# ScalarE's and VectorE's order fixed around the last gate's first group, and a later place for the third output quarter's turn

## The chip, the cores and the metric

One Trainium2 chip, one core of it. The metric is the device time of one execution in microseconds; the kernel before takes 816.92 us, the median of 3 runs (816.7 to 817.8). Five engines work side by side, each on its own list of instructions in its own order: TensorE (PE in the profile), VectorE (DVE), ScalarE (ACT), GpSimd (POOL) and SyncE (SP), which issues most DMAs. They wait for each other through semaphores.

## The reference

One layer of a decoder trunk on 256 tokens of width 2048, in float32:

```
h = rmsnorm(x);  u = h @ w_in            # 2048 x 12288, ten fields
ya = b_g * conv3(c_g * xa) * silu(za);   yb = headnorm(hgrn2(q, f, iv)) * silu(og)
m = sigmoid(ga) * (ya @ w_a_out) + sigmoid(gb) * (yb @ w_b_out)
x = x + m @ w_o
gate = sigmoid(rmsnorm(x) @ w_ple_gate)
x = x + gate * (p @ w_ple_proj)
return rmsnorm(x) * final_norm_g
```

What bears on the change are the last two products: `m @ w_o` (called O below) and `rmsnorm(x) @ w_ple_gate` (called PG), each 256 x 2048 by 2048 x 2048.

## The kernel before

**Products.** TensorE gets float32 accuracy out of three passes. Every operand is cut into a high part, rounded to the type the fast pass takes, and the low rest. `cut` (line 195 on ScalarE, line 196 on VectorE) makes `whi` = the rounded copy of `raw` and `wlo` = `raw` - `whi`; `put` (lines 319 and 320) does the same for the activations and gives `xh` and `xl`. Lines 1122 to 1124 are the three passes: whi with xh, wlo with xh, whi with xl. Each is a matmul of 128 x 128 by 512 columns.

**Items.** All weights stand in one list, `items`. An ordinary item is a piece of 256 x 512 weights: 2 slices of 128 rows x 2 halves of the tokens x 3 passes = 12 matmuls. The main loop takes one item per step, `pos`. A step first writes down the cut of the item `LEAD` = 3 places ahead (some more later on), then the 12 matmuls of its own item, then the DMA issues of loads still further ahead, and then advances every epilogue by one piece (`advance`). An epilogue (`ep_o`, `ep_pg` and so on) is a generator: whatever stands up to its next `yield` is written down in this step. So a `yield` more is one step later.

**Buffers of the cuts.** Pairs of whi and wlo come from two rings (`free_pair`): four pairs that serve all along and five more from a pool `late`, which opens at step `gate`. A cut into one of the four waits until TensorE is done with the item that had the pair.

**O and its epilogue.** O has four groups, one for each quarter of 512 output columns, 8 items each. `ep_o(j)` adds the two psum banks of quarter j to the residual x (line 879, VectorE, two instructions), squares it for the norm (line 880, ScalarE, two) and copies it with its blocks reordered (line 886, ScalarE, two). `turned` then turns the quarter, as PG needs the features on the partitions: four stores to DRAM (line 350, SyncE), one step later the load back (line 361, SyncE), `lag` steps later the block transpose (line 354, VectorE). `put` follows: four xh and four xl, one for each 128 features. So quarter j gives the slices 4j to 4j + 3 of `x1T`, the operand of PG.

**PG and its first group.** PG's first two column quarters are taken together, as one group of 14 items, which begins at step `gate`. Of the 8 slices of 256 features, six are taken plainly, with two items each. The slices 3 and 5 (`LATE_SEVEN`) are combined: seven block products in place of eight, from sums of the activations and of the weights. `late_sums` makes the activations' sums: line 747 joins xh and xl, line 790 makes four differences and sums, `cut` splits them into `shi` and `slo`. Slice 5 belongs to the third quarter of O, so its late sums follow that quarter's turn. `combine_late` makes the sums of the weights (line 747 on `raw`, the cuts `bhi`, `blo` and two more pairs); `settled` is the step of slice 5's item, the tenth of the group. The products P1, P5, P6, P7 stand in four psum banks called g, the corrections in four called s. `ep_products`, written down at step `settled` + 2, takes them out: line 756 copies P1 (ScalarE), lines 747, 758, 747 and 760 combine P6, P5 and P7 (VectorE). The fourth group of O is the one just ahead of `gate`, so its squares, its turn and the third quarter's late sums all fall into the first steps of PG.

**Order.** Where nothing else is said, the scheduler behind the kernel's program may move an engine's instructions past each other by its own estimate of times. `pinned(mark)` takes that freedom away for the two engines that make the cuts: from this step's instructions on, each of ScalarE's and each of VectorE's is tied behind the one written down before it. Line 1304 says for which steps. Before the change these are the steps from `begun` to `parked` + 8, earlier in the program, and `gate` to `settled`. The last steps of O and the steps behind `settled` are free.

Of the kernel before, what the change touches and what calls it, by code (L numbers as in the profile page):

```python
# [48 lines left out]
def hybrid_kernel(ctx, tc, xT, x, pT, prm, gfin, masks, w_in, w_a, w_b, w_o, w_pg, w_pp, out):  # L49
# [32 lines left out]
    def t4(tag="t4", bufs=None):  # L82
        bufs = bufs or {"tmp1": 8, "tmp2": 1, "tmp3": 5}[state["tmp"]]
        return pools[state["tmp"]].tile([P, 1024], F32, tag=tag, bufs=bufs, name=nm(tag))
# [4 lines left out]
    def sc(n, tag="sc", bufs=12):  # L89
        return small.tile([P, n], F32, tag=tag, bufs=bufs, name=nm(tag))  # L90
# [154 lines left out]
    gate = next(n for n, it in enumerate(items) if it["op"] == "x1T")  # L245
    settled = max(n for n, it in enumerate(items) if it["kind"] == "S")
    parked = next(n for n, it in enumerate(items) if it["kind"] == "A" and it["j"] == 3)
    begun = next(n for n, it in enumerate(items) if it["kind"] == "ga" and it["last"])
# [56 lines left out]
    def gain(base, k):  # L305
        return prm_t[:, base + k : base + k + 1]
# [5 lines left out]
    def put(op, k, src, scale=None):  # L312

        hi, lo = op[0][:, k, :], op[1][:, k, :]
        if scale is None:
            nc.scalar.activation(out=hi, in_=src, func=AF.Copy)
            nc.vector.tensor_tensor(out=lo, in0=src, in1=hi.bitcast(F32), op=ALU.subtract)
        else:
            nc.scalar.activation(out=hi, in_=src, func=AF.Identity, scale=scale)  # L319
            nc.vector.scalar_tensor_tensor(  # L320
                out=lo, in0=src, scalar=scale, in1=hi.bitcast(F32), op0=ALU.mult, op1=ALU.subtract
            )


    def rsqrt_of(ss, n, width, tag):

        v = sc(n, tag + "v", 2)
        nc.vector.tensor_scalar(
            out=v, in0=ss, scalar1=1.0 / width, scalar2=EPS, op0=ALU.mult, op1=ALU.add
        )  # L330
        r = sc(n, tag + "r", 2)
        nc.gpsimd.tensor_tensor(out=r, in0=v, in1=mhalf[:, :n], op=ALU.pow)
        return r

    def blocks(ap):

        return ap.rearrange("p (c b e) -> p c b e", b=4, e=32)

    def spread(ap, t):

        return ap.rearrange("p (b c t e) -> p t c b e", b=4, c=4, t=NT)[:, t]

    def to_dram(src, tag, bufs, queue=nc.sync):
        d = dram.tile([P, 4, T], F32, tag=tag, bufs=bufs, name=nm(tag))
        to = d.rearrange("(b i) a x -> a i b x", b=4)
        for a in range(4):
            queue.dma_start(out=to[a], in_=src[32 * a : 32 * a + 32, :].rearrange("i (b x) -> i b x", b=4))  # L350
        return d

    def square_turn(dst, src):
        nc.vector.transpose(
            out=dst.rearrange("p (k a e) -> p a k e", a=4, e=32), in_=src.rearrange("p (a k e) -> p a k e", a=4, e=32)
        )

    def turned(src, lag, dst=None, queues=(nc.sync, nc.sync)):
        d = to_dram(src, "turn", 3, queues[0])
        yield  # L360
        queues[1].dma_start(out=src, in_=d.rearrange("p a x -> p (a x)"))
        for _ in range(lag):
            yield
        dst = t4() if dst is None else dst
        square_turn(dst, src)
        return dst
# [507 lines left out]
    def ep_o(j, psum):  # L874
        xs = state["x"]
        src = t4()
        for t in range(NT):
            d = xs[:, t, j * CW : (j + 1) * CW]
            nc.vector.tensor_tensor(out=d, in0=d, in1=psum[t], op=ALU.add)
            nc.scalar.activation(  # L880
                out=src[:, t * CW : (t + 1) * CW], in_=d, func=AF.Square,
                accum_out=state["ss2"][:, t * 4 + j : t * 4 + j + 1],
            )
        x1 = src
        for t in range(NT):
            nc.scalar.activation(
                out=spread(x1, t), in_=blocks(xs[:, t, j * CW : (j + 1) * CW]), func=AF.Copy
            )
        x1 = yield from turned(x1, 3 if j < 3 else 7)
        for c in range(4):  # L890
            put(state["x1T"], j * 4 + c, x1[:, c * T : (c + 1) * T], gain(PRM_GPLE, j * 4 + c))
        for c in LATE_SEVEN:
            if c // 2 == j:
                yield
                yield from late_sums(c)
        if j == 3:
            tot = sc(2, "tot2", 1)
            nc.vector.tensor_reduce(
                out=tot, in_=state["ss2"].rearrange("p (t j) -> p t j", t=NT),
                axis=mybir.AxisListType.X, op=ALU.add,  # L900
            )
            state["rstd2"] = rsqrt_of(tot, NT, D, "r2")

    def late_sums(c):
        if "late sums" not in state:
            n = len(LATE_SEVEN)
            both = pair_of(pools["tmp3"], 1, ("shi", "slo"), n * 4 * P)
            state["late sums"] = tuple(v.rearrange("p (u s t) -> p u s t", u=n, s=4) for v in both)
        f = t4()
        F, Sv = f[:, :CW].rearrange("p (r b t) -> p r b t", r=2, b=2), f[:, CW:].rearrange("p (s t) -> p s t", s=4)  # L910
        hi, lo = (v[:, 2 * c : 2 * c + 2, :] for v in state["x1T"])
        add(F.rearrange("p r b t -> p r (b t)"), hi.bitcast(F32), lo.bitcast(F32))
        yield
        sums_of(F[:, 0, 0], F[:, 1, 0], F[:, 0, 1], F[:, 1, 1], [Sv[:, i] for i in range(4)])
        yield
        cut(*(v[:, LATE_SEVEN.index(c)] for v in state["late sums"]), Sv)
        yield
# [76 lines left out]
    def ep_last(t, halves):  # L994
# [7 lines left out]
    epilogues = {  # L1002
        "f": ep_f, "q": ep_q, "iv": ep_iv, "og": ep_og, "c": ep_c, "xa": ep_xa, "za": ep_za, "b": ep_b,
        "ga": ep_ga, "gb": ep_gb, "A": ep_a, "B": ep_bb, "O": ep_o, "PG": ep_pg, "PP": ep_pp,
    }

# [92 lines left out]
    def step(e):  # L1099

        a, v = state["splits"]
        with tc.issue_after(a), tc.issue_after(v):
            try:
                next(e)
            except StopIteration:
                active.remove(e)
# [66 lines left out]
    def pinned(start):  # L1173
        traced = nc.cur_bb.bb.instructions
        for engine in (i.engine for i in state["splits"]):
            chain = [i for i in traced[max(start - 400, 0) :] if i.engine == engine]
            fresh = {i.name for i in traced[start:]}
            for a, b in zip(chain, chain[1:]):
                if b.name in fresh:
                    tc.add_manual_dep(  # L1180
                        b, a.name,
                        mybir.DependencyInfo(mybir.DependencyClass.NoSync, mybir.DependencyReason.DATA),
                        reason="order",
                    )
# [6 lines left out]
    for pos, it in enumerate(items[:last_group]):  # L1191
        mark = len(nc.cur_bb.bb.instructions)
        kind, j, c, last = (it[n] for n in ("kind", "j", "c", "last"))
# [99 lines left out]
        if last and kind not in ("S", "C"):  # L1293
# [7 lines left out]
            if not (kind == "f" and j == 0):  # L1301
                active.append(epilogues[kind](j, psum))
                step(active[-1])
        if begun < pos < parked + 8 or gate <= pos <= settled:
            pinned(mark)


# [96 lines left out]
```

## Time and profile before

| what | us |
|---|---|
| runs | 816.92, 816.7, 817.8 |
| profiled execution, its own time | 817.08 |
| its span, first to last instruction | 815.3 |
| TensorE busy, all matmuls | 803.5 |
| VectorE busy | 606.2 |
| ScalarE busy | 462.8 |
| last matmul of 512 columns before the two end pieces begins | 794.65 |

The mean granted clock of TensorE is 0.996. A row of the timeline gives the start and length in us, the engine, the line, the operation with out<-in, how many such instructions follow each other, and in brackets the idle time ahead of the first with what ended it. A suffix q after an engine's name is its queue of DMA issues.

### The profile page before, as it was taken

The page shows a single profiled execution, that of the slowest core. Times are in us where ns is not written, and L with a number is a line of the kernel's source. Part 1 is how long each engine was busy: PE and PEld are TensorE (multiplying, and loading weights), DVE is VectorE, ACT ScalarE, POOL GpSimd, SP SyncE. Part 2 cuts the span into 40 slices and gives each one's busy share as a digit, 9 for nine tenths or more (in the row PEclk, how much of TensorE's full clock was granted, in tenths as well). Part 3 has the DMA queues.
Part 4 walks back from the last instruction along what each step waited for, and adds up shares of the span by engine and source line. Part 5 has one row for each costly group of instructions (what it writes and reads, how often), then busy time and mean ns, then how long its engine had stood idle before and what let it go on. Part 6 is the DMA issues. An engine that isn't in the chain of part 4 may idle for free.

```text
span 815.3 us, 10701 instructions
## 1 busy us (share of the span) xinstructions
PE 803.5 (99%) x4053; PEld 663.9 (81%) x4053; DVE 606.2 (74%) x780; ACT 462.8 (57%) x624; POOL 59.5 (7%) x58
## 2 busy tenths in 40 slices
PE   9999999999999999999999999999999999999995
PEld 6888888888888888888888888888888888877885
DVE  6746588767765498767679878878987656788962
ACT  7576476465555466456455555556545455665733
POOL 1000000001000000000021210201000000000280
PEclk9999999999999999999999999999999999999998
DMA  9988565648767555648799996996845769884822
GB/s 331 391 310 289 196 207 166 236 137 275 249 236 252 193 177 199 207 156 270 259 337 297 320 296 218 324 297 214 249 156 193 281 235 342 291 286 172 317 78 103
DMA packets 53811, 198.52 MB, mean 243 GB/s; under 512 B 6912, under 2 KB 16384, under 8 KB 40064
## 3 DMA queue, kind: packets, MB, share of 16 engines
q1 hardware_dynamic: 44352, 174.78, 60.8%
q0 software_dynamic: 6384, 16.25, 8.3%
q10 hardware_dynamic: 3024, 6.82, 2.5%
q8 instruction: 31, 0.51, 0.3%
q14 instruction: 20, 0.16, 0.1%
HBM read 184.19 MB, written 13.63 MB: 243 GB/s over the span
## 4 chain that ended last, share of the span: by engine, by line
PE 95%; issue 1%; DVE 1%; ACT 1%; POOLq 0%; POOL 0%; ACTq 0%
PE g L1122 27%; PE g L1124 27%; PE g L1123 27%; PE s L1123 4%; PE s L1124 4%; PE s L1122 4%; PE s L530 1%; ACT whi L195 0%; PE s L1014 0%; ACT xh L319 0%; DVE wlo L196 0%; PE s L631 0%; PE s L650 0%; PE s L649 0%; PE s L648 0%
## 5 line engine op out<-in xcount | busy, mean ns | idle before, releaser
L196 DVE TENSOR_TENSOR wlo<-raw,whi 128x1024 fp32r<-128x1024 f32 (+1 forms) x266 | 318.4, 1214 | 151.1 <-ACT whi L195 149.3
L195 ACT ACTIVATE whi<-raw 128x1024 fp32r<-128x1024 f32 (+1 forms) x266 | 274.0, 1049 | 201.4 <-PE g L1124 168.3
L1122 PE MATMUL g<-whi,xh 128*128 128x512 f32 (+1 forms) x676 | 260.0, 385 | 0.0
L1124 PE MATMUL g<-whi,xl 128*128 128x512 f32 (+1 forms) x676 | 259.7, 384 | 0.0
L1123 PE MATMUL g<-wlo,xh 128*128 128x512 f32 (+1 forms) x676 | 259.6, 384 | 0.0
L1122 PEld LDWEIGHTS g<-whi,xh 128*128 128x128 f32 x676 | 127.0, 188 | 25.2
L1124 PEld LDWEIGHTS g<-whi,xl 128*128 128x128 f32 x676 | 127.0, 188 | 25.1
L1123 PEld LDWEIGHTS g<-wlo,xh 128*128 128x128 f32 x676 | 127.0, 188 | 24.9
L1123 PE MATMUL s<-wlo,xh 128*128 128x512 f32 x136 | 53.1, 390 | 0.5 <-DVE wlo L196 0.5
L1124 PE MATMUL s<-whi,xl 128*128 128x512 f32 x136 | 53.0, 390 | 0.0
L1122 PE MATMUL s<-whi,xh 128*128 128x512 f32 x136 | 52.5, 391 | 0.5 <-ACT xh L319 0.4
L1123 PE MATMUL g<-wlo,mh 128*128 128x512 f32 x128 | 49.8, 389 | 0.0
L1124 PE MATMUL g<-whi,ml 128*128 128x512 f32 x128 | 49.8, 390 | 0.0
L1122 PE MATMUL g<-whi,mh 128*128 128x512 f32 x128 | 49.5, 389 | 0.0
L195 ACT ACTIVATE thi<-sA 128x1024 fp32r<-128x1024 f32 x15 | 15.9, 1062 | 32.3 <-DVE sA L747 20.1
L1122 PEld LDWEIGHTS s<-whi,xh 128*128 128x128 f32 x136 | 25.5, 188 | 6.4 <-ACT xh L319 0.8
L1123 PEld LDWEIGHTS s<-wlo,xh 128*128 128x128 f32 x136 | 25.5, 188 | 6.3 <-DVE wlo L196 1.0
L1124 PEld LDWEIGHTS s<-whi,xl 128*128 128x128 f32 x136 | 25.5, 188 | 5.5 <-DVE xl L320 0.2
L1124 PEld LDWEIGHTS g<-whi,ml 128*128 128x128 f32 x128 | 24.0, 188 | 5.2 <-DVE ml L830 0.3
L1122 PEld LDWEIGHTS g<-whi,mh 128*128 128x128 f32 x128 | 24.0, 188 | 5.0
L1123 PEld LDWEIGHTS g<-wlo,mh 128*128 128x128 f32 x128 | 24.0, 188 | 5.0
L1124 PE MATMUL g<-whi,ybTl 128*128 128x512 f32 x64 | 24.9, 389 | 0.0
(243 smaller groups left out, 981.6 us busy)
## 6 DMA issues: line engine op xcount, KB each, us to landing
raw<-in_w_in SPq DMA_DIRECT2D x66, 1024.0 KB, 4.9
raw<-in_w_o SPq DMA_DIRECT2D x16, 1024.0 KB, 6.0
sT<-in_w_in POOLq DMA_DIRECT2D x30, 512.0 KB, 9.2
raw<-in_w_in SPq DMA_DIRECT2D x28, 512.0 KB, 6.1
raw<-in_w_a SPq DMA_DIRECT2D x8, 1024.0 KB, 8.4
raw<-in_w_b SPq DMA_DIRECT2D x8, 1024.0 KB, 8.4
raw<-in_w_pg SPq DMA_DIRECT2D x16, 512.0 KB, 6.0
raw<-in_w_pg SPq DMA_DIRECT2D x8, 1024.0 KB, 6.9
```

Source lines behind the costliest of these rows:

```text
L195: a = nc.scalar.activation(out=hi, in_=src, func=AF.Copy)
L196: v = nc.vector.tensor_tensor(out=lo, in0=src, in1=hi.bitcast(F32), op=ALU.subtract)
L530: nc.tensor.matmul(out, X[:, 0, h, s], X[:, 1, h, t], start=True, stop=True, tile_position=(0, i * n))
L1122: nc.tensor.matmul(psum, oh, hi, start=first, stop=False)
L1123: nc.tensor.matmul(psum, oh, lo, start=False, stop=False)
L1124: nc.tensor.matmul(psum, ol, hi, start=False, stop=last)
```

## The change

Two lines. The third quarter (j = 2) gets six steps instead of three between the load back of its turn and its transpose, with the `put`s and the late sums behind it. And the second stretch of pinned steps grows at both ends: it begins six steps ahead of `gate` and ends two steps behind `settled`.

```
@@ -886,7 +886,7 @@
-        x1 = yield from turned(x1, 3 if j < 3 else 7)
+        x1 = yield from turned(x1, (3, 3, 6, 7)[j])
@@ -1301,7 +1301,7 @@
-        if begun < pos < parked + 8 or gate <= pos <= settled:
+        if begun < pos < parked + 8 or gate - 6 <= pos <= settled + 2:
             pinned(mark)
```

No instruction is added or removed on any engine; GpSimd's order is the same, SyncE's and TensorE's nearly so.

ScalarE, from the cut of step gate's own item on (`whi_5998` before, `whi_5986` now; then gate+1 and gate+2, and the last whi in both lists is gate+3's). `xh` is the third quarter's, the rows of lines 880 and 886 are the fourth's, `shi` is the late sums' cut. Before:

```order
L195 ACTIVATE whi_5998<-raw_5930 128x1024
L195 ACTIVATE whi_6021<-raw_5930 128x1024
L195 ACTIVATE whi_6039<-raw_5967 128x1024
L319 ACTIVATE xh_5648<-t_1034_5970,prm_t 128x256 x4
L880 ACTIVATE t_1046_6058,ss_958_5502<-xs 128x512 x2
L886 ACTIVATE t_1046_6058<-xs 128x4x4x32
L195 ACTIVATE shi_5819<-t_1037_5996 128x512
L886 ACTIVATE t_1046_6058<-xs 128x4x4x32
L195 ACTIVATE whi_6074<-raw_5967 128x1024
```

Now:

```order
L195 ACTIVATE whi_5986<-raw_5930 128x1024
L195 ACTIVATE whi_6005<-raw_5930 128x1024
L319 ACTIVATE xh_5648<-t_1041_6021,prm_t 128x256 x4
L195 ACTIVATE whi_6031<-raw_5967 128x1024
L880 ACTIVATE t_1046_6052,ss_958_5502<-xs 128x512 x2
L886 ACTIVATE t_1046_6052<-xs 128x4x4x32 x2
L195 ACTIVATE whi_6068<-raw_5967 128x1024
```

The third quarter's xh moved ahead of the cut of gate+2, and shi moved behind the cuts of gate+3 and gate+4 (the latter, `whi_6102`, is not shown).

VectorE at the same place, from the wlo of gate+1 (`wlo_6022`, `wlo_6006`). L354 and L320 are the third quarter's, L747 and L790 its late sums, L879 the fourth quarter's. Before:

```order
L196 TENSOR_TENSOR wlo_6022<-raw_5930,whi_6021 128x1024
L196 TENSOR_TENSOR wlo_6040<-raw_5967,whi_6039 128x1024
L879 TENSOR_TENSOR xs<-xs,g_5899 128x512
L879 TENSOR_TENSOR xs<-xs,g_5900 128x512
L354 STREAM_TRANSPOSE t_1034_5970<-t_1020_5883 128x4x8x32
L320 SCALAR_TENSOR_TENSOR xl_5649<-t_1034_5970,prm_t,xh_5648 128x256 x4
L747 TENSOR_TENSOR t_1037_5996<-xh_5648,xl_5649 128x512
L790 TENSOR_TENSOR t_1037_5996<-t_1037_5996 128x128 x4
L196 TENSOR_TENSOR slo_5820<-t_1037_5996,shi_5819 128x512
L196 TENSOR_TENSOR wlo_6075<-raw_5967,whi_6074 128x1024
L196 TENSOR_TENSOR wlo_6105<-raw_6014,whi_6104 128x1024
```

Now:

```order
L196 TENSOR_TENSOR wlo_6006<-raw_5930,whi_6005 128x1024
L354 STREAM_TRANSPOSE t_1041_6021<-t_1020_5883 128x4x8x32
L320 SCALAR_TENSOR_TENSOR xl_5649<-t_1041_6021,prm_t,xh_5648 128x256 x4
L196 TENSOR_TENSOR wlo_6032<-raw_5967,whi_6031 128x1024
L747 TENSOR_TENSOR t_1045_6050<-xh_5648,xl_5649 128x512
L879 TENSOR_TENSOR xs<-xs,g_5899 128x512
L879 TENSOR_TENSOR xs<-xs,g_5900 128x512
L196 TENSOR_TENSOR wlo_6069<-raw_5967,whi_6068 128x1024
L790 TENSOR_TENSOR t_1045_6050<-t_1045_6050 128x128 x4
L196 TENSOR_TENSOR wlo_6103<-raw_6002,whi_6102 128x1024
L196 TENSOR_TENSOR slo_5820<-t_1045_6050,shi_5819 128x512
```

The transpose moved from behind gate+2's wlo and the two L879 to ahead of gate+2's wlo; L790 and slo moved behind the wlo of gate+3.

ScalarE at the group's end: line 756 (P1 out of its bank), the fourth quarter's xh, the whi of slice 5's weight sums (`whi_6266`, `whi_6270`) and those of the next group, PG 2 (`whi_6333` to `whi_6380`). Before:

```order
L195 ACTIVATE whi_6223<-raw_6157 128x1024
L756 ACTIVATE t_1109_6359<-g_6080 128x512
L319 ACTIVATE xh_5648<-t_1087_6250,prm_t 128x256 x4
L195 ACTIVATE whi_6266<-raw_6138 128x1024
L195 ACTIVATE whi_6270<-raw_6138 128x1024
```

Now, the same piece, and further on where line 756 has gone:

```order
L195 ACTIVATE whi_6223<-raw_6157 128x1024
L319 ACTIVATE xh_5648<-t_1087_6250,prm_t 128x256 x4
L195 ACTIVATE whi_6266<-raw_6138 128x1024
L195 ACTIVATE whi_6270<-raw_6138 128x1024
...
L195 ACTIVATE whi_6355<-raw_6306 128x1024
L756 ACTIVATE t_1109_6359<-g_6074 128x512
L195 ACTIVATE whi_6380<-raw_6306 128x1024
```

Line 756 moved from ahead of the fourth quarter's xh to behind the third cut of PG 2; on VectorE the line 747 that follows it moved behind the wlo of that cut (`wlo_6356`), and lines 758 and 747 behind the next one.

## Prediction

> **What bounds the kernel now.** The page first. Its first part:
>
> ```profile
> PE 803.5 (99%) x4053; PEld 663.9 (81%) x4053; DVE 606.2 (74%) x780; ACT 462.8 (57%) x624; POOL 59.5 (7%) x58
> ```
>
> TensorE is the bound, and the 99% hides how well it is fed, since a matmul of 512 columns is shown 0.39 us long but follows the one ahead of it closer than that. So the table by stretches comes next, read by the count of matmuls behind PE's busy time (the columns: us, busy us and count of PE, PEld, DVE, ACT, POOL, then PE's clock, the share and GB/s of DMA):
>
> ```profile
> 720.00:725.00 5.00, 5.00 (x24) 3.99 (x22) 3.69 (x10) 4.53 (x11) 0.00 (x0) 1.00 0.37 125
> 725.00:730.00 5.00, 4.42 (x19) 3.15 (x18) 4.69 (x5) 5.00 (x7) 0.00 (x0) 1.00 0.94 309
> 745.00:750.00 5.00, 4.17 (x17) 2.42 (x15) 2.58 (x7) 3.83 (x7) 0.71 (x1) 1.00 0.00 0
> 750.00:755.00 5.00, 4.79 (x22) 3.88 (x22) 5.00 (x5) 5.00 (x6) 0.00 (x0) 1.00 0.44 144
> 755.00:760.00 5.00, 5.00 (x24) 4.14 (x23) 5.00 (x7) 2.02 (x3) 0.00 (x0) 1.00 0.96 362
> ```
>
> A full stretch shows 24 matmuls; 725 to 730 lacks 5, 745 to 755 lacks 7 and 2. The clock column stays at 1.00. The timeline of PE shows where they are missing, with the waits in brackets:
>
> ```profile
> 716.91 0.39 PE L1122 MATMUL s<-whi,xh 128*128 128x512 f32 x1
> ...
> 725.29 0.73 PE L1122 MATMUL s<-whi,xh 128*128 128x512 f32 x2
> 726.55 0.50 PE L1123 MATMUL s<-wlo,xh 128*128 128x512 f32 x1 [0.53 <-DVE wlo L196]
> ...
> 734.41 0.39 PE L1122 MATMUL s<-bhi,shi 128*128 128x512 f32 x1
> ...
> 747.22 0.50 PE L1122 MATMUL s<-whi,xh 128*128 128x512 f32 x1 [0.40 <-ACT xh L319]
> ...
> 749.37 0.51 PE L1122 MATMUL g<-whi,shi 128*128 128x512 f32 x1 [0.43 <-ACT whi L195]
> ...
> 750.32 0.73 PE L1122 MATMUL g<-whi,shi 128*128 128x512 f32 x2 [0.21 <-ACT whi L195]
> ```
>
> Item `gate` begins at 716.91. An ordinary item is 12 matmuls and takes 2.72 us (0.2267 each), as the two whi rows at 711.67 and 714.39 below show: each is let go when an item ends. Six items later, at 716.91 + 6 x 2.72 = 733.23, the first combined item should begin; it does at 734.41. **First loss: 1.18 us**, at item gate+3. Fourteen missing matmuls x 0.2267 are 3.17 us in all, so the **second loss is about 1.99 us**. The whole change can win 3.2 us, 0.4%, if the rest of the order holds.
>
> Why they happen is in the timelines of ScalarE and VectorE. ScalarE:
>
> ```profile
> 700.22 0.62 ACT L880 ACTIVATE t<-xs 128x512 f32<-128x512 f32 x1
> ...
> 702.02 1.04 ACT L195 ACTIVATE whi<-raw 128x1024 fp32r<-128x1024 f32 x1
> ...
> 711.67 1.06 ACT L195 ACTIVATE whi<-raw 128x1024 fp32r<-128x1024 f32 x1 [1.66 <-PE g L1124]
> 714.39 1.06 ACT L195 ACTIVATE whi<-raw 128x1024 fp32r<-128x1024 f32 x1 [1.66 <-PE g L1124]
> 719.10 1.71 ACT L319 ACTIVATE xh<-t,prm_t 128x256 fp32r<-128x256 f32 x4 [3.64 <-DVE t L354]
> 720.71 0.61 ACT L880 ACTIVATE t<-xs 128x512 f32<-128x512 f32 x1
> ...
> 724.20 3.89 ACT L195 ACTIVATE whi<-raw 128x1024 fp32r<-128x1024 f32 x4
> ...
> 746.17 0.60 ACT L756 ACTIVATE t<-g 128x512 f32<-128x512 f32 x1 [8.24 <-PE g L1124]
> 746.67 1.70 ACT L319 ACTIVATE xh<-t,prm_t 128x256 fp32r<-128x256 f32 x4
> 748.26 6.74 ACT L195 ACTIVATE whi<-raw 128x1024 fp32r<-128x1024 f32 x7
> 756.62 2.01 ACT L195 ACTIVATE whi<-raw 128x1024 fp32r<-128x1024 f32 x2 [1.61 <-DMA raw<-in_w_pg]
> ```
>
> VectorE:
>
> ```profile
> 712.77 1.23 DVE L196 TENSOR_TENSOR wlo<-raw,whi 128x1024 fp32r<-128x1024 f32 x1 [1.49 <-ACT whi L195]
> 715.49 1.23 DVE L196 TENSOR_TENSOR wlo<-raw,whi 128x1024 fp32r<-128x1024 f32 x1 [1.50 <-ACT whi L195]
> 716.63 1.28 DVE L879 TENSOR_TENSOR xs<-xs,g 128x512 f32<-128x512 f32 x2
> 717.83 1.24 DVE L354 STREAM_TRANSPOSE t<-t 128x1024 f32<-128x1024 f32 x1
> 719.64 1.68 DVE L320 SCALAR_TENSOR_TENSOR xl<-t,prm_t,xh 128x256 fp32r<-128x256 f32 x4 [0.58 <-ACT xh L319]
> 721.36 0.69 DVE L747 TENSOR_TENSOR t<-xh,xl 128x512 f32<-128x512 f32 x1
> 722.09 1.02 DVE L790 TENSOR_TENSOR t<-t 128x128 f32<-128x128 f32 x4
> 723.80 0.69 DVE L196 TENSOR_TENSOR slo<-t,shi 128x512 fp32r<-128x512 f32 x1 [0.70 <-ACT shi L195]
> 725.27 4.63 DVE L196 TENSOR_TENSOR wlo<-raw,whi 128x1024 fp32r<-128x1024 f32 x4 [0.78 <-ACT whi L195]
> ...
> 743.65 1.24 DVE L354 STREAM_TRANSPOSE t<-t 128x1024 f32<-128x1024 f32 x1
> 747.20 1.69 DVE L320 SCALAR_TENSOR_TENSOR xl<-t,prm_t,xh 128x256 fp32r<-128x256 f32 x4 [2.32 <-ACT xh L319]
> ```
>
> First loss: the cut of gate+3 (724.20, the first of four) stands behind the third quarter's turn, the fourth's squares and the late sums' shi; between 715.45 and 724.20 ScalarE cuts no weights, and PE wants that whi at 716.91 + 3 x 2.72 = 725.07. Second loss: L756 waits 8.24 us for the last product of P1, and the fourth quarter's xh, whose turn was done at 743.65 + 1.24 = 744.89, stands behind it until 746.67. The xh, the two whi of the last combined item and PE's waits at 747.22, 749.37 and 750.32 follow in one chain.
>
> **The change, part by part.** No instruction is added or removed; the cost is all in the order. I rebuild both engines' new order with the spacings of the rows.
>
> Start: wlo of gate+1 at 712.77; two wlo stand 1.14 apart. The turn L354 now comes next, at 713.91. Its data must be there:
>
> ```profile
> 708.97 0.33 SPq L361 DMA_DIRECT2D t<-turn  x1
> ...
> DMA to landing us min/median/max: 4.1/4.1/4.1
> ```
>
> The load back (the second row is line 361 alone from 708 to 710) lands at 713.1, and SyncE's order ahead of it is unchanged, so 0.8 us to spare. L354 to xh is 1.27 (717.83 to 719.10): xh at 715.18; four xh take 1.61 (719.10 to 720.71): whi of gate+2 at 716.79, where it was 714.39; PE wants it at 722.35, so this slip costs nothing. Its wlo 1.10 later (714.39 to 715.49), 717.89; L747 at 719.03; the two L879, 0.6 apart, at 719.64, long after the O products' end, which is where `gate` begins. ScalarE's first L880 follows at 720.35, the second at 720.97, and from the second to the next whi is 1.80 (700.22 to 702.02): **whi of gate+3 at 722.77 instead of 724.20**, ready 723.83 against 725.07. Its wlo starts at 723.87 and is ready at 725.09; PE, which issues two whi matmuls first, wants it at 725.53. The first loss goes, with 0.44 us to spare on VectorE.
>
> The price stands behind that wlo: L790 x4 (0.94: 1.02 less the 0.08 by which neighbours overlap) and slo (0.60, as two L879: 1.28 less one of 0.69), which were done earlier, now come among the wlo. The fourth wlo of that run started at 725.27 + 3 x 1.14 = 728.68; now at 723.87 + 1.14 + 0.94 + 1.14 + 0.60 + 1.14 = 728.83. So VectorE, which ran without a pause from there to 744.89, is **0.14 us later**, while PE is 1.18 earlier: the operands' lead shrinks by 1.3 us. The tightest on that stretch is the first combined item's whi that waits for VectorE's sums: it starts at 733.50 (below), is ready at 734.56 and used by PE at 737.13. Of these 2.6 us 1.3 remain: covered.
>
> ```profile
> 733.50 2.96 ACT L195 ACTIVATE whi<-raw 128x1024 fp32r<-128x1024 f32 x3 [3.00 <-DVE raw L747]
> ...
> 737.13 0.39 PE L1122 MATMUL g<-whi,shi 128*128 128x512 f32 x1
> ```
>
> Second loss: L756 now stands nine rows later, behind the third whi of PG 2, the group that follows on PE. The last L354 starts at 743.65 + 0.14 = 743.79, xh 1.27 later at **745.06 instead of 746.67: 1.61 us earlier**. The whi behind it, VectorE's xl and the wlo behind that were bound to xh alone and shift by the same 1.61. PE arrives there 1.18 earlier, hence still waits for them, about 1.99 + 1.18 - 1.61 = 1.56 us. So the gain is not the sum of the two losses but the shift of this chain: **-1.61 us**.
>
> What L756's later place costs: it frees P1's bank, and the L747 behind it P6's, for group PG 2, which starts 186 matmuls after `gate`: 716.91 + 42.2 + 3.2 = 762.3 before, 760.7 after. L756 follows the whi at 756.62, even unshifted: 757.6 to 758.2; its L747 stands behind that whi's wlo and ends near 759.5, and P6's bank is wanted at 761.3. Nothing, with 1.8 us of cover. No transfer is issued later for it: the fourth turn's four stores leave SyncE when the second L886 ends, which is just ahead of the whi of gate+3 in both orders (722.77 against 724.20), and the raw loads queued behind them gain the same 1.4 us.
>
> A rule of the Trainium skill speaks against pinning: in "TensorE: Matmul & The Clock Gate", section "Architectural detail", ScalarE's and VectorE's queues are strictly first in, first out, so a fixed order lets a waiting row hold ready ones. The trace agrees (746.17: 8.24 us of waiting, xh only at its end). By it the new order's own holes are real, and they are in the sum: ScalarE stands about 2.5 us ahead of 720.35, VectorE 3 us ahead of 723.87. If ScalarE could overtake, xh would start at 744.92 already and the sum would be +0.14, not -1.61.
>
> The sum against the profiled execution: 817.08 (span 815.3 and 1.8 around it) - 1.61 = 815.5. The median of the runs is 0.16 lower, so 816.92 - 1.61 = **815.3 us**, -0.2%. Unknown are the small spacings under ScalarE's and VectorE's new neighbours: nine hand-overs at up to 0.05 either way, 0.45 together.
>
> **The rivals.** *Slower.* L354, now fixed ahead of gate+2's cut, waits for a late load back, and both engines stand behind it: every 0.1 us past 713.91 moves the whole chain. All of line 361 between 640 and 760 landed within:
>
> ```profile
> DMA to landing us min/median/max: 4.1/5.1/9.4
> ```
>
> At 9.4 it would land at 718.4, 4.5 us late: PE waits 4.0 at gate+3, the last xh comes at 749.5, 2.85 later than before: 817.08 + 2.85 = 819.9. It decides from a landing of 6.6 us (713.91 + 1.61). For it: the spread. Against: this very load took 4.1 and nothing ahead of it moves. 7%. The Trainium skill, in "TensorE: Matmul & The Clock Gate", section "What's actually happening", halves TensorE's clock after an idle window of about 3.4 us; by it that 4.0 us wait would cost up to 1.7 us more, an estimate from its figure, and no wait here is long enough to show it.
>
> *No gain that shows.* Something else holds the last combined item's whi: its weights' sums, or a later stage. Against: the sums end ahead of 743.65, and further on the operands are far ahead of PE (the whi at 756.62 is PG 2's third, wanted at 762.3 + 2 x 2.72 = 767.7). The time would be 816.4 to 817.1. 10%.
>
> *Both losses go*: PE meets ready operands everywhere, 817.08 - 3.17 = 813.9. Against: xh cannot come ahead of 745.06 with VectorE without a pause from 723.87. 8%.
>
> **How the numbers follow.** The forecast case, a gain of 1.0 to 2.2 us, has 75%. The bound of 0.2%, about what a measurement of this kernel can tell from no change, is 1.63 us, so this case splits evenly on it. Faster 0.38 + 0.08, rounded to 0.46; same 0.37 + 0.10 = 0.47; slower 0.07. The range 814.4 to 816.6 takes the forecast with 0.45 of hand-overs and 0.4 of the runs' spread to either side and the better part of the smaller gains; it leaves out the slower case, half of the no-gain case and most of the both-go case, some 17%.
>
> **What would show it.** Right: 725 to 730 holds 24 matmuls; whi of gate+3 starts near 722.8; no wait at 725; xh of the fourth quarter near 745.1 straight behind L354, L756 near 755 to 758; PE still waits for whi at about 747.7. Wrong: L354 waiting for a DMA after 713.9; a PE wait on wlo near 725.5; a wait for the g bank near 761; a VectorE run that ends well after 745.

## The result and the profile after

| kernel | median us | runs, lowest to highest |
|---|---|---|
| before | 816.77 | 22, 816.24 to 817.80 |
| changed | 815.55 | 22, 814.65 to 817.65 |

The ratio is 0.9986, with a 95% interval of 0.9979 to 0.9992: faster by 1.2 us, a little under the forecast 1.61. The profiled execution has 815.29 us of its own time and a span of 813.5 us, at a mean granted clock of 0.998.

The page's first part, after, has 1.2 us less on TensorE and differs by at most 0.8 us elsewhere:

```profile
PE 802.3 (99%) x4053; PEld 663.2 (82%) x4053; DVE 607.0 (75%) x780; ACT 463.0 (57%) x624; POOL 59.9 (7%) x58
```

The same stretches as before (us, busy us and count of PE, PEld, DVE, ACT, POOL, PE's clock, DMA share, GB/s):

```profile
720.00:725.00 5.00, 5.00 (x24) 3.95 (x22) 2.06 (x4) 4.39 (x8) 0.00 (x0) 1.00 0.47 109
725.00:730.00 5.00, 5.00 (x23) 4.13 (x23) 4.93 (x9) 4.15 (x6) 0.00 (x0) 1.00 1.01 359
745.00:750.00 5.00, 4.14 (x16) 2.51 (x16) 4.40 (x9) 5.00 (x8) 0.72 (x1) 1.00 0.00 0
750.00:755.00 5.00, 5.00 (x24) 4.14 (x23) 5.00 (x5) 3.44 (x5) 0.00 (x0) 1.00 0.81 288
```

725 to 730, which lacked five matmuls, is busy throughout, with 23 where a full stretch shows 24. 745 to 750 still lacks eight. TensorE's timeline, with the first matmul of `gate` and what is left of the waits:

```profile
716.32 0.39 PE L1122 MATMUL s<-whi,xh 128*128 128x512 f32 x1
...
724.94 0.50 PE L1123 MATMUL s<-wlo,xh 128*128 128x512 f32 x1
725.28 0.40 PE L1124 MATMUL s<-whi,xl 128*128 128x512 f32 x1
...
745.40 0.50 PE L1122 MATMUL s<-whi,xh 128*128 128x512 f32 x1 [0.20 <-ACT xh L319]
...
747.55 0.50 PE L1122 MATMUL g<-whi,shi 128*128 128x512 f32 x1 [0.44 <-ACT whi L195]
...
748.50 0.73 PE L1122 MATMUL g<-whi,shi 128*128 128x512 f32 x2 [0.22 <-ACT whi L195]
```

At gate+3 (724.94) there is no bracket any more; only the next matmul comes 0.34 us later instead of 0.2267, so about 0.1 us of the first loss is left. Of the three waits of the second loss the one for xh is halved (0.40 before) and the other two are as they were. ScalarE at these places:

```profile
715.01 1.71 ACT L319 ACTIVATE xh<-t,prm_t 128x256 fp32r<-128x256 f32 x4 [2.87 <-DVE t L354]
716.62 1.05 ACT L195 ACTIVATE whi<-raw 128x1024 fp32r<-128x1024 f32 x1
...
722.59 1.99 ACT L195 ACTIVATE whi<-raw 128x1024 fp32r<-128x1024 f32 x2
...
744.84 1.71 ACT L319 ACTIVATE xh<-t,prm_t 128x256 fp32r<-128x256 f32 x4 [6.99 <-DVE t L354]
...
755.71 0.58 ACT L756 ACTIVATE t<-g 128x512 f32<-128x512 f32 x1
...
793.32 0.84 ACT L963 ACTIVATE t<-g,r2r 128x256 f32<-128x256 f32 x2 [4.33 <-PE g L1124]
```

The fourth quarter's xh (744.84) now waits for its own turn L354 and for nothing else; L756 has gone to 755.71. VectorE:

```profile
712.17 1.23 DVE L196 TENSOR_TENSOR wlo<-raw,whi 128x1024 fp32r<-128x1024 f32 x1 [1.50 <-ACT whi L195]
713.73 1.25 DVE L354 STREAM_TRANSPOSE t<-t 128x1024 f32<-128x1024 f32 x1 [0.33 <-DMA t<-turn]
...
723.66 1.23 DVE L196 TENSOR_TENSOR wlo<-raw,whi 128x1024 fp32r<-128x1024 f32 x1 [2.94 <-ACT whi L195]
...
743.57 1.24 DVE L354 STREAM_TRANSPOSE t<-t 128x1024 f32<-128x1024 f32 x1
```

The third quarter's L354 (713.73) has a bracket that the forecast did not have: it waits for its DMA. The load back's issue, and its landing:

```profile
708.53 0.33 SPq L361 DMA_DIRECT2D t<-turn  x1
...
DMA to landing us min/median/max: 5.2/5.2/5.2
```

It took 5.2 us, where the profile of before had 4.1.

**Where the time went.** Executions differ by some tenths in when `gate` begins (716.91 before, 716.32 after), and not by the change: two experiments below with before's order at that place, e7 and e1, begin it at 716.39 and 717.11. So I count from the first matmul of `gate` to the first row of line 963 on ScalarE, the sigmoid on the first of the two end pieces. The row of before:

```profile
795.13 0.84 ACT L963 ACTIVATE t<-g,r2r 128x256 f32<-128x256 f32 x2 [4.68 <-PE g L1124]
```

That is 795.13 - 716.91 = 78.22 us before and 793.32 - 716.32 = 77.00 after: **1.22 us less**, the same as the medians. Of the 3.17 us that before lost, 3.17 - 1.22 = 1.95 are still lost.

### The profile page after: what moved, and what is told of

Read it like the earlier page. It is cut to its first block, busy times and chain, and to the rows that moved or that the text cites. A ratio compares the mean times of both kernels' runs of the same rounds, so it can differ in the third digit from the quotient of the medians.

```text
span 813.5 us, 10701 instructions
## 1 busy us (share of the span) xinstructions
PE 802.3 (99%) x4053; PEld 663.2 (82%) x4053; DVE 607.0 (75%) x780; ACT 463.0 (57%) x624; POOL 59.9 (7%) x58
## 4 chain that ended last, share of the span: by engine, by line
PE 96%; issue 1%; ACT 1%; DMA 0%; DVE 0%; POOLq 0%; POOL 0%; ACTq 0%
PE g L1122 27%; PE g L1124 27%; PE g L1123 27%; PE s L1123 4%; PE s L1124 4%; PE s L1122 4%; PE s L530 1%; DMA praw<-in_pT 0%; ACT whi L195 0%; PE s L631 0%; PE s L650 0%; PE s L649 0%; PE s L648 0%; ACT xs L985 0%; ACT xh L319 0%
## 5 line engine op out<-in xcount | busy, mean ns | idle before, releaser
L1122 PE MATMUL g<-whi,yaTh 128*128 128x512 f32 x64 | 24.9, 389 | 0.0
```

Of the source, the lines that this page charges most:

```text
L1122: nc.tensor.matmul(psum, oh, hi, start=first, stop=False)
```

## The experiments

Two theories stand in the expectations. **A**: the two losses hang together in one chain, the time follows the fourth quarter's xh, and only its shift counts. **B**: the two losses are separate and what is saved at each adds up. Later expectations speak of **A2**, which is A with one more term: the gain is 1.6 us less the delay of the third quarter's L354 behind its slot. For each kernel the median of its runs is given with the ratio to before, run on the same chip, and its 95% interval; before's median was 816.86 us beside e1 to e4, 816.70 beside e5 to e8 and 816.97 beside e9 to e11 (26 to 28 runs each).

### e1: the far end alone

```
-        if begun < pos < parked + 8 or gate <= pos <= settled:
+        if begun < pos < parked + 8 or gate <= pos <= settled + 2:
```

> Only the far end of the change: pinned from gate to settled + 2, the third turn at its old place. Theory A (one chain: the time follows the start of the fourth quarter's xh): the first loss of 1.2 us at gate+3 stays, xh starts at the end of its transpose, 744.92 where it was 746.67, so -1.7 us, more than the whole change gave. Theory B (two losses that add up: the far end is worth what the whole change has beyond the first loss): -0.1 us at most, since the whole gave 1.2 and the first loss alone is 1.2.

815.05 us (814.92 to 815.57, 11 runs), ratio 0.998 [0.9972, 0.9989]. The profile, first the waits of TensorE in this part of the program, then the fourth quarter's xh and L756:

```profile
PE s L1123 <- DVE wlo L196: 0.5, 1, 0.5
```

```profile
745.12 1.71 ACT L319 ACTIVATE xh<-t,prm_t 128x256 fp32r<-128x256 f32 x4 [5.83 <-DVE t L354]
...
755.93 0.58 ACT L756 ACTIVATE t<-g 128x512 f32<-128x512 f32 x1
```

The first loss stays whole (the wait for wlo at gate+3 is the one of before), and still this third of the change is worth 1.8 us, no less than the whole. Since TensorE still comes to the second place 1.2 us late, the operands are there: no wait for xh or whi is shown there any more. B falls.

### e2: the near end and the later turn, without the far end

```
-        x1 = yield from turned(x1, 3 if j < 3 else 7)
+        x1 = yield from turned(x1, (3, 3, 6, 7)[j])
-        if begun < pos < parked + 8 or gate <= pos <= settled:
+        if begun < pos < parked + 8 or gate - 6 <= pos <= settled:
```

> The near end and the third turn's later place alone: pinned from gate - 6 to settled. Theory A: the first loss goes, line 756 still stands ahead of the fourth quarter's xh and waits for TensorE, which now comes 1.2 us earlier, so xh starts 1.2 us earlier: -1.2 us, or 0.1 to 0.2 less if the turn's load back lands after VectorE is free for it. Theory B: -1.2 us too. Both: no wait on wlo at gate+3, a wait for xh as long as before near the fourth quarter's slices.

816.04 us (815.42 to 818.07, 11 runs), 0.9993 [0.9984, 1.0002]: not told apart from before by its runs. The profiled execution's ScalarE at the second place:

```profile
744.78 0.60 ACT L756 ACTIVATE t<-g 128x512 f32<-128x512 f32 x1 [6.96 <-PE g L1124]
745.27 1.70 ACT L319 ACTIVATE xh<-t,prm_t 128x256 fp32r<-128x256 f32 x4
```

L756 stands ahead of xh again, but it waits only 6.96 us where it waited 8.24: the first loss is gone, so P1 is done 1.2 us sooner after `gate`, and xh with it (716.70 to 745.27 is 28.57 us, before 29.76). This is how the two losses hang together: the first one delays P1, P1 holds L756, L756 holds xh. Either end of the change shortens that one chain. They do not add up because xh starts at the later of two times: the end of its own turn L354, and the end of L756. L354 starts 26.74 us after `gate` before and in e1 and 26.83 in e2, so neither end brings it earlier, and the far end alone already leaves nothing else to wait for.

### e3: both ends, the third quarter's turn at its old three steps

```
-        x1 = yield from turned(x1, (3, 3, 6, 7)[j])
+        x1 = yield from turned(x1, 3 if j < 3 else 7)
```

(as against the changed kernel)

> The whole pinned stretch, but the third quarter's turn after three steps as before, so that its transpose is fixed ahead of gate-1's wlo. Both engines must stand there until the load back lands (713.1 to 713.7 on the clock of before): gate-1's whi comes at 716.0 to 716.6 behind four xh where TensorE wants it at 714.2, its wlo is ready at 718.3 to 718.9 where it is wanted at 714.6, 3.7 to 4.3 us lost there. Later losses go almost wholly, since the late sums are done early. Theory A: 3.2 won, 3.7 to 4.5 lost, +0.5 to +1.4 us. If the load's landing does not hold the engines (the 0.42 us at this transpose after the change have another cause): -2 us or more.

819.15 us (818.92 to 820.88, 6 runs), 1.0033 [1.0021, 1.0045]: **slower** by 2.3 us, more than the expected 0.5 to 1.4. VectorE:

```profile
712.65 1.25 DVE L354 STREAM_TRANSPOSE t<-t 128x1024 f32<-128x1024 f32 x1 [7.42 <-DMA t<-turn]
```

L354 is tied into an order in which its load has not landed, and waits 7.42 us with both cutting engines behind it. TensorE runs dry one item ahead of `gate`:

```profile
713.35 0.39 PE L1124 MATMUL g<-whi,ml 128*128 128x512 f32 x1
716.63 0.73 PE L1122 MATMUL g<-whi,mh 128*128 128x512 f32 x2 [2.89 <-ACT whi L195]
717.89 0.50 PE L1123 MATMUL g<-wlo,mh 128*128 128x512 f32 x1 [0.53 <-DVE wlo L196]
...
719.01 0.63 PE L1122 MATMUL g<-whi,mh 128*128 128x512 f32 x1
719.44 0.63 PE L1123 MATMUL g<-wlo,mh 128*128 128x512 f32 x1
...
721.57 0.63 PE L1122 MATMUL s<-whi,xh 128*128 128x512 f32 x1
```

Without the wait `gate` would begin at 713.35 + 0.23 + 2.72 = 716.30; it begins at 721.57, 5.27 us later. Gaps account for some 3.9 of them (713.35 to 716.63 less one spacing, and 0.8 at 717.89). The rest is another thing: from 719.01 on matmuls follow each other by 0.43 us, not 0.2267, and the clock column of the stretches shows why:

```profile
710.00:715.00 5.00, 3.74 (x17) 2.77 (x15) 1.77 (x3) 1.07 (x3) 0.00 (x0) 1.00 0.29 103
715.00:720.00 5.00, 2.84 (x9) 1.96 (x10) 4.51 (x8) 3.48 (x5) 0.00 (x0) 0.88 0.22 46
720.00:725.00 5.00, 5.00 (x19) 4.04 (x18) 4.58 (x8) 2.56 (x5) 0.00 (x0) 0.78 1.01 386
```

The granted clock falls to 0.88 and 0.78 of full behind the pause: seven matmuls at 0.43, the last of them `gate`'s first, 1.4 us. The expectation had no such term; without these 1.4 us the loss would lie within it, at an estimated 0.9. Behind `gate` the early turn pays (xh 25.60 us after it, no wait left), and still the sum is a loss. So the near end needs the later turn: without it, both cutting engines stand still for a load.

### e4: the squares of the fourth quarter one step later

```
-        x1 = yield from turned(x1, (3, 3, 6, 7)[j])
+        if j == 3:
+            yield
+        for t in range(NT):
+            d = xs[:, t, j * CW : (j + 1) * CW]
...
+        x1 = yield from turned(x1, (3, 3, 6, 6)[j])
```

(as against the changed kernel; the yield stands between the two L879 and the squares, with the loop over t split in two)

> The whole change, and the fourth quarter's squares and copies (lines 880 and 886) one step later than its two additions, with one step less before its transpose; so the cut of gate+3 stands ahead of them. Theory A: that cut's wlo starts right behind the two additions, 3 us earlier than now; VectorE's run without a pause to the last transpose begins and ends as much earlier, xh is there before TensorE wants it, and both losses go: about -3 us against before. If transfers hold the late raw weights or the turn: -1.2 to -2 us, with waits of whi or of the transpose for DMA. Theory B has no more than -1.2 to -1.6 us.

814.06 us (813.56 to 815.57, 11 runs), 0.9969 [0.9961, 0.9978]: 2.8 us below before's median, where the change itself has 1.2. The execution that was profiled was its slowest, 815.57. VectorE, SyncE's queue, and the landing:

```profile
716.09 1.25 DVE L354 STREAM_TRANSPOSE t<-t 128x1024 f32<-128x1024 f32 x1 [2.45 <-DMA t<-turn]
```

```profile
701.79 3.29 SPq L350 DMA_DIRECT2D turn<-t  x4
...
710.53 0.33 SPq L361 DMA_DIRECT2D t<-turn  x1
```

The third quarter's four stores took 3.29 us to issue, the load back went out 6.03 us ahead of `gate` (716.56; 7.79 in the changed kernel) and held L354 for 2.45 us. Take these 2.45 off this run's time, down to what TensorE needs without a wait, and an estimate of 813.6 comes out, the time of its fastest runs (716.56 + 75.05 of full stretch + 21.96 behind it = 813.57). That the other runs between 813.6 and 815.6 differ by this landing is likely from that, but they left no trace.

### e5: the load back one step later, its turn one step shorter

```
-        yield
+        for _ in range(1 + hold):
+            yield
...
-        x1 = yield from turned(x1, (3, 3, 6, 7)[j])
+        x1 = yield from turned(x1, (3, 3, 5, 7)[j], hold=j == 2)
```

(as against the changed kernel)

> The whole change, but the third turn's load back is issued one step later and the transpose keeps its place in the order, so the load lands later behind more raw loads, by perhaps 1.5 to 4 us. Theory A2 (the gain is 1.6 us less the time by which the third quarter's transpose starts after VectorE is free for it): with the transpose d us late, -1.6 + d; for d of 2 to 4 us +0.4 to +2.4 us, with that wait shown on VectorE as one for the load. If the landing does not set the time: -1.2 us as the change itself.

815.77 us (814.72 to 817.02, 11 runs), 0.9989 [0.998, 0.9998]. The edit missed its aim, since SyncE isn't pinned and its load still went out at the old place, 716.60 - 708.93 = 7.67 us ahead of `gate`:

```profile
708.93 0.33 SPq L362 DMA_DIRECT2D t<-turn  x1
```

So this is a second profile of the changed order, and useful as that: here the load landed in 3.8 us, L354 did not wait, and `gate` to line 963's row took 76.59 us. That is 1.63 less than before, the 1.61 of the forecast.

### e6: the later turn alone

```
-        x1 = yield from turned(x1, 3 if j < 3 else 7)
+        x1 = yield from turned(x1, (3, 3, 6, 7)[j])
```

> The third turn's later place alone, pinned as before. The scheduler keeps the transpose behind the fourth quarter's two additions, near 717.8 on the clock of before, well after the landing, but the late sums' differences stand behind gate+3's wlo, as after the change. Theory A: the first loss goes, line 756 stays ahead of xh and comes 1.2 us earlier with TensorE: -1.2 us; and, as the load back can land 4 us later without harm, the runs lie as close together as those of the far end alone (0.7 us) and not spread over 3 us. If the spread of the changed kernel is not from the landing, this one spreads as much.

815.75 us (815.19 to 816.02, 11 runs), 0.9988 [0.9979, 0.9997]. ScalarE:

```profile
722.93 1.99 ACT L195 ACTIVATE whi<-raw 128x1024 fp32r<-128x1024 f32 x2
...
744.86 0.60 ACT L756 ACTIVATE t<-g 128x512 f32<-128x512 f32 x1 [6.66 <-PE g L1124]
745.36 1.69 ACT L319 ACTIVATE xh<-t,prm_t 128x256 fp32r<-128x256 f32 x4
```

The later turn alone takes shi behind the cut of gate+3 (722.93) and so ends the first loss, as in e2 and with the same gain in the profile; the earlier pin has no part in it. And as VectorE's steps ahead of `gate` stay free here, L354 keeps its old place and no load is late: the runs spread by 0.8 us, where e2's spread by 2.7.

### e7 and e8: the squares later, with the far end alone and with a turn of seven steps

e7, as against before, has e1's line, e4's yield and

```
-        x1 = yield from turned(x1, 3 if j < 3 else 7)
+        x1 = yield from turned(x1, 3 if j < 3 else 6)
```

e8 is e4 with

```
-        x1 = yield from turned(x1, (3, 3, 6, 6)[j])
+        x1 = yield from turned(x1, (3, 3, 7, 6)[j])
```

> The far end alone, third turn at its old place, and the fourth quarter's squares and copies one step later than its additions, one step less before its transpose. The transpose of the third quarter stays near 717.8, so the landing has no say; the cut of gate+3 stands ahead of xh and squares, the first loss goes, and the last transpose comes about 1.1 us earlier. Theory A: -2.4 to -2.8 us and runs within about 0.8 us of each other. Theory B: -1.2 us.

> The whole pinned stretch, the squares one step later as in e4, and the third turn after seven steps, so its transpose stands behind gate+2's wlo and is wanted at 716.6 on the clock of before, 2.7 us later than after the change. Theory A2: landings up to 7.6 us after the issue cost nothing now; -2.2 to -2.6 us with runs close together, where e4 had a part of its runs 1.5 us above its fastest.

e7: 814.26 us (814.01 to 814.58, 7 runs), 0.9971 [0.996, 0.9982]. e8: 814.50 us (814.20 to 815.12, 9 runs), 0.9974 [0.9964, 0.9984]. What TensorE waits for in this part, and the place of gate+3's whi in e7:

```profile
PE g L1126 <- ACT whi L195: 0.2, 1, 0.2
```

```profile
716.36 1.06 ACT L195 ACTIVATE whi<-raw 128x1024 fp32r<-128x1024 f32 x1 [1.43 <-PE g L1127]
...
743.68 1.71 ACT L319 ACTIVATE xh<-t,prm_t 128x256 fp32r<-128x256 f32 x4 [6.98 <-DVE t L354]
```

With the squares a step later the cut of gate+3 comes ahead of the third quarter's xh, at 716.36, L354 has its late place of before, where no load holds it, and the fourth xh comes 27.29 us after `gate`. Of the 3.17 us that before lost, 0.69 remain (75.74 us to line 963's row). Both ends' aims are reached without the near pin, and the runs lie within 0.6 us. Against their own runs of before e7 gains 2.4 us, e8 2.2 and e4 2.8; the intervals overlap, and e4's runs spread by 2.0.

### e9 and e10: the load back held behind the cut of `gate`, and of gate+1

Both have both ends of the change; in `turned` the third quarter's load back is written down later and tied behind the whi of `gate` (e9) or of gate+1 (e10). Its slot for L354 stays.

```
-        yield
-        queues[1].dma_start(out=src, in_=d.rearrange("p a x -> p (a x)"))
+        for _ in range(1 + hold):
+            yield
+        back_in = queues[1].dma_start(out=src, in_=d.rearrange("p a x -> p (a x)"))
+        if hold:
+            tc.add_manual_dep(back_in.ins, state["splits"][0].name, ...)
...
-        x1 = yield from turned(x1, (3, 3, 6, 7)[j])
+        x1 = yield from turned(x1, (3, 3, 1, 7)[j], hold=5 if j == 2 else 0)
```

(e10: lag 0 and hold 6)

> e5 again with an edit that holds: the third turn's load back waits for ScalarE's whi of item gate (its end is at 710.0 on the clock of before) and stands behind two more raw loads on SyncE, so it is issued 1 to 1.5 us later and may land 4 to 7 us after that, 714.4 to 717. ScalarE's and VectorE's order is that of the changed kernel. Theory A2 (gain = 1.6 less the transpose's delay past 713.9): with the delay d shown by the trace, -1.6 + d, so -1.1 to +1.5 us, and in the profiled execution the stretch from the first matmul of gate to the end's first sigmoid is 78.22 - 1.6 + d. If the landing does not set the time: -1.2 us.

> The same with the load back behind ScalarE's whi of gate+1 (its end at 712.7 on the clock of before), landing near 716.9 to 718. Theory A2: d of 3.0 to 4 us, so +1.4 to +2.4 us, slower than before: the slower rival's mechanism at full size, with a PE wait on whi and wlo at gate+3 and TensorE's wait for the fourth quarter's xh behind it. If the landing does not set the time: -1.2 us.

e9: 817.68 us (816.99 to 818.25, 11 runs), 1.001 [1.0001, 1.0019]. e10: 817.97 us (817.20 to 818.84, 11 runs), 1.0013 [1.0004, 1.0022]. Both are slower than before, by 0.7 and 1.0 us in the median. VectorE of e9:

```profile
715.74 1.25 DVE L354 STREAM_TRANSPOSE t<-t 128x1024 f32<-128x1024 f32 x1 [2.13 <-DMA t<-turn]
```

VectorE of e10, and what TensorE then waits for at gate+3:

```profile
716.99 1.25 DVE L354 STREAM_TRANSPOSE t<-t 128x1024 f32<-128x1024 f32 x1 [3.24 <-DMA t<-turn]
```

```profile
PE s L1128 <- ACT whi L195: 1.9, 1, 1.9
```

Reckoned from `gate`, the slot of L354 in this order is -3.00 us (e2 and e5, where it waits for nothing). In e9 it starts at -0.79, 2.21 late, in e10 at +0.32, 3.32 late. A2 gives 78.22 - 1.61 + 2.21 = 78.82 us from `gate` to line 963's row, measured 78.80; and for e10 79.93, measured 79.94. In these two profiles every 0.1 us of a late landing costs 0.1 us. e10's profiled execution (818.57, 1.72 us more from `gate` to line 963's row) lies in the expected 1.4 to 2.4; its median, 1.0 above before's, does not, and the other executions have no trace that would say when their loads landed.

### e11: e9's load back in e8's order

e8 with e9's tie, `(3, 3, 2, 6)` for the lags and `hold=5` for the third quarter.

> Control for e9: the same later load back (behind the whi of gate) in e8, where the transpose is wanted at 716.6 instead of 713.9. Theory A2: a landing of 714.4 to 716.6 costs nothing, up to 0.4 us if it is later: -2.2 us as e8, or -1.8. If a later load costs time for another reason than the transpose's place (transfers that it shifts), about as much is lost here as in e9.

815.00 us (814.57 to 816.76, 11 runs), 0.9979 [0.997, 0.9988], 2.0 us below its own before, where e8 has 2.2. The profiled execution was its slowest:

```profile
718.64 1.25 DVE L354 STREAM_TRANSPOSE t<-t 128x1024 f32<-128x1024 f32 x1 [0.53 <-DMA t<-turn]
```

The load landed 7.2 us after its issue, L354 came 0.33 after `gate` (718.31) where e8's came 0.29 ahead of it, and the stretch is 76.49 against e8's 75.88: 0.61 for a delay of 0.62. That `gate` itself began 1.9 us later here is not the turn's: 1.0 us of it is a wait for a blo at 475 us, much earlier in the program. The rest was not traced.

## Why the prediction was nearly right

All executions together first, from their rows: the start of `gate`, then, counted from it, the fourth quarter's xh on ScalarE and line 963's row.

| kernel | `gate` | fourth xh | line 963 | difference of the two |
|---|---|---|---|---|
| before | 716.91 | 29.76 | 78.22 | 48.46 |
| changed | 716.32 | 28.52 | 77.00 | 48.48 |
| e1 | 717.11 | 28.01 | 76.49 | 48.48 |
| e2 | 716.70 | 28.57 | 77.05 | 48.48 |
| e4 | 716.56 | 28.58 | 77.05 | 48.47 |
| e5 | 716.60 | 28.11 | 76.59 | 48.48 |
| e6 | 716.72 | 28.64 | 77.10 | 48.46 |
| e7 | 716.39 | 27.29 | 75.74 | 48.45 |
| e8 | 716.37 | 27.40 | 75.88 | 48.48 |
| e9 | 716.53 | 30.32 | 78.80 | 48.48 |
| e10 | 716.67 | 31.42 | 79.94 | 48.52 |
| e11 | 718.31 | 28.02 | 76.49 | 48.47 |
| e3 | 721.57 | 25.60 | 75.39 | 49.79 |

- **"The gain is not the sum of the two losses but the shift of this chain": right.** In the first twelve executions the last column is the same within 0.07 us, while the fourth xh moves over 4.1 us. Only e3 leaves the rule, where xh is so early that TensorE itself bounds: 78.22 - 3.17 = 75.05 us is its own need, and `gate`'s first two matmuls, still at the lower clock, add 0.3.
- **"L354 at 713.91 ... 0.8 us to spare": this is the step that failed.** In the changed profile its load went out 7.79 us ahead of `gate` instead of 7.94 and took 5.2 us instead of 4.1, so L354 started 2.59 us ahead of `gate` instead of 3.00, 0.41 late. The 0.8 came from one execution's 4.1 us, though the same view showed 4.1 to 9.4 for this line; I took the one number for this load and should have put its spread into the sum. With that term the sum is -1.61 + 0.41 = -1.20, and the profile has -1.22. That the medians differ by 1.22 too is luck to this decimal: the same order gained 1.63 in e5's profile, and the changed kernel's runs spread by 3.0 us. So is a part of how near the time of 815.3 us came to 815.55: before's median over 22 runs lies 0.15 below that of the three it was counted from.
- **"The first loss goes, with 0.44 us to spare on VectorE": right but for about 0.1 us.** whi of gate+3 came 6.27 us after `gate` (5.86 forecast), its wlo was ready at 724.89 and used at 724.94, and the matmul behind that came 0.11 late. The 0.41 of the late load ate the spare.
- **"VectorE is 0.14 us later" and "xh 1.27 behind L354": right, apart from the late load.** The last L354 stands 27.25 after `gate` against 26.88 forecast, and xh 28.52 against 28.15, both 0.37 later and so within the 0.41 of the late load; 743.57 to 744.84 is 1.27.
- **"PE still waits, 1.56 us": right in kind**, 1.95 measured, of which 0.4 is the late load.
- **L756's later place costs nothing: right.** It starts at 755.71, and no wait for a g bank is seen near 761.
- **The spacings under new neighbours, 0.45 either way:** with the late load in, they sum to 0.02.
- **The slower rival** was a real mechanism with the right price, in a small dose. Its turning point, 6.6 us behind an issue 7.94 ahead of `gate`, is a landing 1.34 ahead of `gate`. The changed kernel's landed 2.59 ahead, faster than before; e9's about 0.8 ahead, slower. As far as profiles show, it may also explain why the median gain is 1.2 and not 1.6: over the nine executions in which the load was not held back (e3 apart, whose `gate` was), it landed from 3.87 to 0.53 us ahead of `gate`, and behind the slot of -3.00 in four. Orders whose L354 waits at that slot spread by 2.0 to 3.0 us over their runs (changed, e2, e4, e5), those with the later place by 0.6 to 0.9 (e1, e6, e7, e8), before by 1.1 to 1.7. The kernels whose load is held do not divide like this: e9 and e10, with the slot, spread by 1.3 and 1.6, e11, with the later place, by 2.2. That the spread of the runs comes from the landing is thus likely and not shown.
- **The no-gain rival** fell: nothing else holds the last combined item. **Both losses going** was right to be kept small for this change; e7 shows what it takes.
- **The rule of the Trainium skill on first in, first out** ("TensorE: Matmul & The Clock Gate", section "Architectural detail") was the right one to weigh: e3 is its price paid in full, 7.42 us of L354 with both engines' cuts behind it: the whi of gate-1, which before's order makes at 706.23, comes at 715.54.

So of the change's three parts, the far end alone gives 1.8 us and the later turn alone 1.0. On top of the later turn the near end gives nothing (e2 against e6: 77.05 and 77.10 us to line 963's row); it puts a DMA's landing into the chain and takes back 0.4 in the changed profile. The far end with the later turn and without the near end was not run.

## What to carry to other kernels

When two waits of one engine are found, look whether the first delays what the second waits for: here either remedy shortened the same chain, and the whole change was worth no more than its better half. Before an instruction that waits for a DMA is tied into an engine's order, take the spread of that DMA's landing over all its issues, not the one in the profile; what lies behind the tied slot goes one for one into the time, and likely into the scatter of the runs. Measure a small change from a fixed event in the program (here the first matmul of a group), since the work ahead of it moves by some tenths from execution to execution.

## What the runs showed of the hardware that was not expected

**A pause lowers TensorE's clock afterwards.** In e3 waits of 2.89 and 0.53 us, with two matmuls between them, were followed by seven matmuls at 0.43 us instead of 0.2267, beginning 5.7 us after the start of the last matmul ahead of the pause (713.35 to 719.01), and then by full speed: 1.4 us on top of the waits. In e10's profile a wait of 1.9 us was followed by no such thing (its clock column stays at 1.00). But over all executions the mean granted clock was 0.992 to 0.995 in e3, 0.994 in three of e9's eleven and in four of e10's, and 0.996 to 0.998 in every other execution on record. So the clock may have fallen in some executions of e9 and e10 too; they left no trace. The Trainium skill, in "TensorE: Matmul & The Clock Gate", section "What's actually happening", has half the clock after an idle window of about 3.4 us. The half clock agrees (0.2267 / 0.43 = 0.53); that a pause broken by two matmuls is enough is shown by e3's profile alone.

**The same load lands in 3.8 to 7.2 us.** The third quarter's load back, of one size, took 3.8 to 5.5 us in the ten profiles in which it was not held: 4.1 before, 5.2 after, 3.8 in e2 and e5, 5.5 in e4. Held behind a cut, it took 6.1 in e9, 4.4 in e10 and 7.2 in e11. What sets it was not tried.
